# A hybrid attention block on one core: where the weights' sums, the tokens' sums and the rows of x are asked for

## The chip, the core and the metric

The kernel runs on one core of a Trainium2 chip. The core has a matrix engine (PE, with its weight loads as PEld), a vector engine (DVE), a scalar engine (ACT), GpSimd (POOL) and SyncE (SP), which here only issues transfers. The metric is the device time of one execution in microseconds (us); less is better.

## What is computed

One layer of a streaming encoder, 512 tokens, width 2048, eight stick-breaking heads and eight latent heads, all float32. Cut to what matters:

```
h = rms_norm(x, pre_norm_w)
sb_q, sb_k, sb_v, sb_gate, c_q, c_kv, k_rope, mla_gate = split(h @ w_in)
# stick-breaking heads (8 x 128), strictly causal
z = q @ k.T * scale
a[t,s] = sigmoid(z[t,s]) * prod_{s<j<t} (1 - sigmoid(z[t,j]))
o_a = a @ v
# latent heads (8): queries and keys by low-rank factors, rotary part, chunk-causal softmax
o_b = softmax(mask(q_mla @ k_mla.T * scale)) @ v_mla
mixed = concat([o_a * silu(sb_gate), o_b * silu(mla_gate)])     # 512 x 2048
y = mixed @ w_out                                               # 512 x 2048
out = x + rms_norm(y, post_norm_w)
```

## The kernel before, in words

**Products.** A float32 product is made of three products of parts: `split` (L94) makes a rounded part on ACT (L96, tiles ending in h or hi) and the remainder on DVE (L99, ending in l or lo), and `mm3` (L127) issues three matmuls (L122). `weights` (L104) brings a 128 x 1024 piece of a weight by a load on SP (L88, tile raw, four buffers) and splits it into whi and wlo (three buffers each).

**Order.** PE's matmuls and SP's loads are kept in the order of the code. On DVE, ACT and POOL a scheduler puts the instructions in an order by the place in the code and by when it takes their inputs to be ready, unless the code pins one with `keep_in_program_order`. Once built, each engine works through its list in order, so an instruction that waits holds all behind it.

**The run.** First the norm and the low-rank projections; then eight latent heads (to about 310 us), then eight stick-breaking heads (to about 700 us). A generator, `filler`, fills PE between the steps of the heads with the projections of the heads to come and, in the end, with the output product. In a stick-breaking head k is scaled (kr) and split (kh, kl); for each of four blocks b of 128 tokens there follow the scores z on PE, a mask on z (DVE, L885), two sigmoids (ACT, L887 the first), a scan (DVE, prod, L889), and a product (DVE, beta, L891). PE then transposes beta (tp) and multiplies it with v (av). The gated head, mix (L745), is put into DRAM by POOL (`put_aside`, L749) and comes back by `split_mixed` (POOL load L392, tile mx, then mxh and mxl).

**The output product.** The columns of w_out come in four groups of 512 for the tokens' four blocks. `out_group(0)` and `out_group(1)` (L433) take the first 1024 columns, eight weights i each with two mixed heads j; their four banks y are emptied by `out_piece`: a sum of squares on ACT (L407) and a product with the post weight on DVE (L416). The second group uses the same banks, so PE waits for L416 of the first. `last_columns` (L517) makes the other 1024 columns with seven products of half the size in place of eight, in the manner of Strassen: A11, S1, S2, S3, A22, A12 and, with weights kept from earlier, S4 (banks sx, sz, sy, sv, sx, sp). It needs sums on both sides:

- weights' sums: `weight_sums(j)` (L461), eight sets, each of four loads of 128 x 512 from w_out (POOL, L466, tile wsum, from a ring qrt of eight slots), four subtractions (DVE, L468) and four stores to DRAM (POOL, L469, tensors w_sums). They are called from the stick-breaking heads but depend on nothing there, and none is pinned;
- tokens' sums: `first_sums(j)` (L476), eight of them, called inside the output groups from the fifth weight of the first one on: two mixed heads again from DRAM (POOL, L473, ring mv of four slots), three sums (L481 to L483), splits (s12, hl4); and `last_sum` (L489), eight, in the second half of the second group.

S3 and A22 share the banks sv and are emptied by `sum_piece` (L419): L423 adds, L407 squares, L425 multiplies. Between A22 and A12, four pieces w22 are loaded and split into kept tiles (woh, wol, halves of 128 x 512) for S4; A12's own pieces are w21. `residual(b)` (L567) loads four pieces of x for a block (SP, tile xr), makes the factor r (L575, L576 on DVE, L578, L579 on POOL), computes x + r*y (L587) and stores it (L588, SP and ACT by turns).

Of the kernel before, what the change touches and what calls it, by code (L numbers as in the profile page):

```python
# [57 lines left out]
def block(ctx: ExitStack, tc: tile.TileContext, a: dict):  # L58
# [10 lines left out]
    def g(name, dt=F32, tag="g"):  # L69
        return gen.tile([P, S], dt, tag=tag, name=name, bufs=SLOTS[tag])  # L70
# [16 lines left out]
    def load(out, in_):  # L87
        tc.keep_in_program_order(nc.sync.dma_start(out=out, in_=in_))  # L88
# [15 lines left out]
    def weights(src, n):  # L104
        raw = ring.tile([P, 1024], F32, tag="raw", name="raw", bufs=N_RAW)
        load(out=raw[:, :n], in_=src)
        hi = ring.tile([P, 1024], F32R, tag="whi", name="whi", bufs=N_HI)
        lo = ring.tile([P, 1024], F32R, tag="wlo", name="wlo", bufs=N_HI)
        split(hi[:, :n], lo[:, :n], raw[:, :n])
        return hi, lo  # L110
# [322 lines left out]
    def out_group(gi):  # L433
        banks = [bank(f"y{b}") for b in range(NB)]
        for i in range(8):
            wh, wl = weights(a["w_o"][gi, i], 1024)
            if i == 0:
                for _ in range(4):
                    split_mixed()
            if 4 <= 8 * gi + i < 12:  # L440
                first_sums(8 * gi + i - 4)
            for j in range(2):
                s_ = slice(j * S, (j + 1) * S)
                split_mixed()
                for b in range(NB):
                    out_mm(banks[b], b, i * 2 + j, wh[:, s_], wl[:, s_])
                    yield
            if gi == 1 and i >= 4:
                last_sum(2 * i - 8)
                last_sum(2 * i - 7)  # L450
        pw = post_weight(gi)
        for b in range(NB):
            out_piece(b, gi * S, banks[b], pw)
# [4 lines left out]
    sums = {}  # L458
    w_sums = [dram.tile([4, P, 1024], F32, name=f"w_sums{n}") for n in range(4)]

    def weight_sums(j):  # L461

        i, c = j // 2, slice((j % 2) * S, (j % 2 + 1) * S)
        b11, b12, b22, b21 = (g("wsum", tag="qrt") for _ in range(4))
        for t, gi, k in ((b11, 2, 0), (b12, 3, 0), (b22, 3, 4), (b21, 2, 4)):
            pool.dma_start(out=t, in_=a["w_o"][gi, k + i][:, c])  # L466
        for n, (out, x, y) in enumerate(((b11, b12, b11), (b12, b22, b12), (b22, b22, b11), (b21, b21, b22))):
            dve.tensor_tensor(out=out, in0=x, in1=y, op=ALU.subtract)  # L468
            pool.dma_start(out=w_sums[n][i][:, c], in_=out)  # L469

    def mixed_again(n):
        t = g("mx", tag="mv")
        pool.dma_start(out=t, in_=mixed[order[n]])  # L473
        return t

    def first_sums(j):  # L476

        x, y = mixed_again(j), mixed_again(j + 8)
        t, s4 = g("st", tag="tr"), g("st4", tag="tr")[:, :HALF]
        s1, s2 = t[:, :HALF], t[:, HALF:]  # L480
        dve.tensor_tensor(out=s1, in0=x[:, HALF:], in1=y[:, HALF:], op=ALU.add)  # L481
        dve.tensor_tensor(out=s2, in0=s1, in1=x[:, :HALF], op=ALU.subtract)
        dve.tensor_tensor(out=s4, in0=y[:, :HALF], in1=s2, op=ALU.subtract)  # L483
        h12, l12, hl4 = g("s12h", F32R), g("s12l", F32R), g("s4", F32R)
        split(h12, l12, t)
        split(hl4[:, :HALF], hl4[:, HALF:], s4)
        sums[j] = h12, l12, hl4

    def last_sum(j):  # L489

        x = mixed_again(j)
        s3 = x[:, HALF:]
        dve.tensor_tensor(out=s3, in0=x[:, :HALF], in1=s3, op=ALU.subtract)
        split(msplit[j][0][:, HALF:], msplit[j][1][:, HALF:], s3)

    def factor(which, j, r):

# [6 lines left out]
        k, c = {"A11": (0, lo_), "S3": (0, hi_), "A12": (8, lo_), "A22": (8, hi_)}[which]  # L504
        return msplit[j + k][0][:, c], msplit[j + k][1][:, c]

    def product(banks, which, srcs, start, stop):
        for i in range(4):
            wh, wl = weights(srcs[i], 1024)
            for j in (2 * i, 2 * i + 1):  # L510
                s_ = slice((j % 2) * S, (j % 2 + 1) * S)
                for r in range(2):
                    mm3(banks[r], *factor(which, j, r), wh[:, s_], wl[:, s_], start and j == 0, stop and j == 7,
                        skip_group_check=True)
                    yield

    def last_columns():  # L517
        w11, w21, w22 = ([a["w_o"][gi, k + i] for i in range(4)] for gi, k in ((2, 0), (2, 4), (3, 4)))
        x = [bank("sx") for _ in range(2)]
        yield from product(x, "A11", w11, True, False)  # L520
        s1 = [g("s1", tag="t") for _ in range(2)]
        s15 = [g("s15", tag="t") for _ in range(2)]
        for r in range(2):
            act.copy(out=s1[r], in_=x[r])
        z = [zbank("sz") for _ in range(2)]
        yield from product(z, "S1", w_sums[0], True, True)
        for r in range(2):
            dve.tensor_tensor(out=s15[r], in0=z[r], in1=s1[r], op=ALU.add)
        y = [tbank("sy") for _ in range(2)]
        yield from product(y, "S2", w_sums[2], True, True)  # L530
        for r in range(2):
            dve.tensor_tensor(out=s1[r], in0=y[r], in1=s1[r], op=ALU.add)
            dve.tensor_tensor(out=s15[r], in0=y[r], in1=s15[r], op=ALU.add)
        pw2, pw3 = post_weight(2, "mv"), post_weight(3, "mv")
        junk = g("junk", tag="mv")
        v = [bank("sv") for _ in range(2)]
        yield from product(v, "S3", w_sums[1], True, False)
        for r in range(2):
            sum_piece(2 + r, 3 * S, v[r], s15[r], pw3, junk)
        yield from product(v, "A22", w_sums[3], False, True)  # L540
        for r in range(2):
            sum_piece(2 + r, 2 * S, v[r], s1[r], pw2, junk)

# [21 lines left out]
            residual(b, b == 1)  # L565

    def residual(b, tail=False):  # L567
        xs = []
        for i in range(4):
            xr = g("xr")  # L570
            load(out=xr, in_=a["x"][b * P:(b + 1) * P, i * S:(i + 1) * S])
            xs.append(xr)
        n = pieces[b]
        part = tn("part")
        dve.tensor_reduce(out=part, in_=ssy[b][:, :n - 1], axis=AX.X, op=ALU.add)  # L575
        dve.tensor_scalar(out=part, in0=part, scalar1=EPS, scalar2=None, op0=ALU.add)  # L576
        r2 = tn("r2")
        pool.tensor_tensor(out=r2, in0=ssy[b][:, n - 1:n], in1=part, op=ALU.add)  # L578
        pool.tensor_tensor(out=r2, in0=r2, in1=mhalf[:, :1], op=ALU.pow)  # L579
        for i, (at, y) in enumerate(sorted(ypw[b].items())):  # L580
            w = y.shape[1]
            o = xs[at // S][:, at % S:at % S + w]
            if tail and i == 2:
                act.activation(out=y, in_=y, func=AF.Copy, scale=r2)
                pool.tensor_tensor(out=o, in0=y, in1=o, op=ALU.add)
            else:
                dve.scalar_tensor_tensor(out=o, in0=y, scalar=r2, in1=o, op0=ALU.mult, op1=ALU.add)  # L587
            (nc.sync, nc.scalar)[i % 2].dma_start(out=a["out"][b * P:(b + 1) * P, at:at + w], in_=o)  # L588
# [283 lines left out]
        fill(max(0, 4 * NK + NK * (h + 2) - taken[0]))  # L872


    for h in range(H):
        kh, kl = need("k", h)
        qh, ql = need("q", h)
        fill(4)
        rows = row_tiles("beta")
        for b in range(NB):  # L880
            n = (b + 1) * P
            w = max(n, 256)
# [7 lines left out]
                                   initial=1.0, op0=ALU.mult, op1=ALU.add)  # L890
            dve.tensor_tensor(out=beta[:, :n - 1], in0=beta[:, :n - 1], in1=prod[:, 1:n], op=ALU.mult)  # L891
            fill((1, 3, 3, 7)[b])
        if h < H - 1:
            weight_sums(h)
        if h == H // 2:
            weight_sums(H - 1)
        cur = Weighted(rows, need("v", h // 4), (h % 4) * P)
        for j in range(NB):
            cur.turn(j)
# [64 lines left out]
```

## Time and profile before

| what | us |
| --- | --- |
| runs | 881.47, 881.5, 883.67; median 881.5 |
| profiled execution | 883.35 |
| span of the profiled execution | 881.3 |
| PE busy | 844.3 (96%) |
| PEld, DVE, ACT, POOL busy | 706.7, 485.3, 360.4, 91.2 |

A profile page gives the busy time of each engine, the span in slices, the transfers and the chain of work that ended last. Behind it the trace can be asked for stretches, waits and single instructions. In a row of the timeline the first number is the start, the second how long it took, then the engine, the line, the operation, the tile written and the tiles read; in brackets stands how long the engine was idle before and what it waited for. A line of waits names the engine with the waiting instruction, then what released it. A granted clock of 1.00 is PE's full speed, 2.4 GHz, and 0.50 is 1.2 GHz.

### The profile page before, as it was taken

How to read it: one execution, taken by the hardware profiler on the slowest of the kernel's cores; microseconds unless marked ns; L12 is line 12 of the kernel's file. 1: busy time of each engine (PE TensorE's matmuls, PEld its weight loads, DVE VectorE, ACT ScalarE, POOL GpSimd, SP SyncE). 2: the span in 40 equal slices, each digit the busy share in tenths (PEclk: the TensorE clock that was granted, in tenths of full speed). 3: DMA queues.
4: the chain of work that ended last, by engine and by line, in shares of the span. 5: the costliest groups of instructions: out<-in, count | busy, mean ns of one | idle time of the engine just before them, and what ended most of it. 6: DMA issues, size and time to landing. Idle time of an engine off the chain costs nothing.

```text
span 881.3 us, 11034 instructions
## 1 busy us (share of the span) xinstructions
PE 844.3 (96%) x4074; PEld 706.7 (80%) x4074; DVE 485.3 (55%) x869; ACT 360.4 (41%) x622; POOL 91.2 (10%) x189
## 2 busy tenths in 40 slices
PE   8999999988899999999999999999999996999993
PEld 6889988876688888888888888888888884888773
DVE  5676656657685543355363524546355666435675
ACT  7652655543444533333242324333244333334541
POOL 1000001134450020000000000000001021000011
PEclk9999999999899999999999999999999997999997
DMA  9822322356782152222323234222223275427677
GB/s 337 323 93 80 122 88 99 105 198 236 235 286 96 60 180 96 96 88 92 101 80 107 73 108 144 96 84 90 90 96 132 94 229 167 142 90 229 197 260 241
DMA packets 41477, 126.84 MB, mean 144 GB/s; under 512 B 5760, under 2 KB 6288, under 8 KB 41424
## 3 DMA queue, kind: packets, MB, share of 16 engines
q1 hardware_dynamic: 29520, 88.75, 30.0%
q0 software_dynamic: 10608, 35.42, 11.8%
q10 hardware_dynamic: 1296, 1.97, 0.6%
q8 instruction: 32, 0.52, 0.3%
q14 instruction: 21, 0.17, 0.1%
HBM read 109.34 MB, written 16.78 MB: 143 GB/s over the span
## 4 chain that ended last, share of the span: by engine, by line
PE 77%; DMA 10%; issue 5%; DVE 4%; ACT 2%; POOL 1%; SPq 1%; DVEq 0%; POOLq 0%; ACTq 0%
PE gps L122 16%; PE qp L122 10%; PE v L122 10%; PE kp L122 10%; PE y L122 6%; PE cq L122 4%; DMA wsum<-in_w_o 4%; PE av L122 3%; DMA xr<-in_x 2%; PE ckv L122 2%; PE sv L122 2%; DMA mx<-mixed 2%; PE mz L122 2%; PE z L122 2%; PE tp L125 2%
## 5 line engine op out<-in xcount | busy, mean ns | idle before, releaser
L99 DVE TENSOR_TENSOR wlo<-raw,whi 128x1024 fp32r<-128x1024 f32 (+2 forms) x137 | 163.3, 1192 | 144.1 <-ACT whi L96 141.3
L96 ACT CAST whi<-raw 128x1024 fp32r<-128x1024 f32 (+2 forms) x137 | 140.5, 1026 | 215.3 <-PE kp L122 42.6
L122 PE MATMUL gps<-hh,whi 128*128 128x512 f32 x256 | 102.9, 402 | 0.0
L122 PE MATMUL gps<-hl,whi 128*128 128x512 f32 x256 | 100.8, 394 | 0.0
L122 PE MATMUL gps<-hh,wlo 128*128 128x512 f32 x256 | 100.8, 394 | 0.0
L122 PE MATMUL y<-whi,mxh 128*128 128x512 f32 x128 | 51.3, 401 | 8.7 <-DVE y L416 8.7
L122 PEld LDWEIGHTS gps<-hh,wlo 128*128 128x128 f32 x256 | 48.5, 189 | 10.8
L122 PEld LDWEIGHTS gps<-hl,whi 128*128 128x128 f32 x256 | 48.8, 191 | 7.8
L122 PEld LDWEIGHTS gps<-hh,whi 128*128 128x128 f32 x256 | 48.6, 190 | 7.7
L96 ACT CAST th<-tp 128x512 fp32r<-128x512 f32 (+1 forms) x64 | 27.1, 423 | 66.0 <-PE tp L125 63.2
L99 DVE TENSOR_TENSOR tl<-tp,th 128x512 fp32r<-128x512 f32 (+1 forms) x64 | 31.2, 487 | 38.7 <-ACT th L96 38.2
L122 PE MATMUL qp<-hh,whi 128*128 128x512 f32 x128 | 52.0, 407 | 0.0
L122 PE MATMUL v<-whi,hh 128*128 128x512 f32 x128 | 50.9, 397 | 0.0
L122 PE MATMUL y<-wlo,mxh 128*128 128x512 f32 x128 | 50.8, 397 | 0.0
L122 PE MATMUL y<-whi,mxl 128*128 128x512 f32 x128 | 50.7, 396 | 0.0
L122 PE MATMUL qp<-hh,wlo 128*128 128x512 f32 x128 | 50.1, 391 | 0.0
L122 PE MATMUL qp<-hl,whi 128*128 128x512 f32 x128 | 50.0, 391 | 0.0
L122 PE MATMUL v<-whi,hl 128*128 128x512 f32 x128 | 49.9, 390 | 0.0
L122 PE MATMUL v<-wlo,hh 128*128 128x512 f32 x128 | 49.9, 390 | 0.0
L122 PE MATMUL kp<-hh,whi 128*128 128x512 f32 x128 | 49.8, 389 | 0.0
L122 PE MATMUL kp<-hl,whi 128*128 128x512 f32 x128 | 49.8, 389 | 0.0
L122 PE MATMUL kp<-hh,wlo 128*128 128x512 f32 x128 | 49.8, 389 | 0.0
(290 smaller groups left out, 1806.8 us busy)
## 6 DMA issues: line engine op xcount, KB each, us to landing
raw<-in_w_t SPq DMA_DIRECT2D x64, 512.0 KB, 3.2
raw<-in_w_o SPq DMA_DIRECT2D x28, 512.0 KB, 3.2
mx<-mixed POOLq DMA_DIRECT2D x39, 256.0 KB, 3.7
wsum<-in_w_o POOLq DMA_DIRECT2D x32, 256.0 KB, 3.7
w_sums<-wsum POOLq DMA_DIRECT2D x32, 256.0 KB, 2.9
raw<-in_w_v SPq DMA_DIRECT2D x16, 512.0 KB, 3.2
raw<-w_sums SPq DMA_DIRECT2D x16, 512.0 KB, 4.3
xs<-in_x SPq DMA_DIRECT2D x16, 256.0 KB, 6.4
```

Of the source, the lines that this page charges most:

```text
L96: i = act.copy(out=hi, in_=src)
L99: dve.tensor_tensor(out=lo, in0=src, in1=hi.bitcast(F32), op=ALU.subtract)
L122: tc.keep_in_program_order(pe.matmul(out=out, lhsT=lhsT, rhs=rhs, start=start, stop=stop, **kw))
L125: tc.keep_in_program_order(pe.transpose(out, in_, identity))
```

## The change

Three things, in one diff.

1. `weight_sums` is cut in two: `load_weight_parts` at the head of a stick-breaking head, the subtractions and stores behind its four blocks; all of it is pinned. Head h has set h, head 4 has set 7 as well. The four sums are stored in another order (the tensors 1 and 2 change places, and S2 and S3 read accordingly).
2. `first_sums` is called two weights earlier in the code, its loads one step ahead of it; the last sums become a generator, `late_sums`, that is stepped beside A11 and S1. Neither is pinned.
3. The rows of x are loaded by `load_x`, a generator stepped beside S3 (blocks 2 and 3) and A22 (blocks 0 and 1): two loads of 256 KB behind each piece of weights, on SP, pinned. `residual` finds them there.

```diff
-            if 4 <= 8 * gi + i < 12:
-                first_sums(8 * gi + i - 4)
+            at = 8 * gi + i - 6
+            if 0 <= at + 1 < H:
+                load_pair(at + 1)
+            if 0 <= at < H:
+                first_sums(at)
...
-            if gi == 1 and i >= 4:
-                last_sum(2 * i - 8)
-                last_sum(2 * i - 7)
...
+    def load_weight_parts(j):
+        i, c = j // 2, slice((j % 2) * S, (j % 2 + 1) * S)
+        w_parts[j] = []
+        for gi, k in ((2, 0), (3, 0), (3, 4), (2, 4)):
+            t = g("wsum", tag="qrt")
+            tc.keep_in_program_order(pool.dma_start(out=t, in_=a["w_o"][gi, k + i][:, c]))
+            w_parts[j].append(t)
+
     def weight_sums(j):
...
+        b11, b12, b22, b21 = w_parts.pop(j)
+        for n, (out, x, y) in ((0, (b11, b12, b11)), (2, (b12, b22, b12)), (1, (b22, b22, b11)), (3, (b21, b21, b22))):
+            tc.keep_in_program_order(dve.tensor_tensor(out=out, in0=x, in1=y, op=ALU.subtract))
+            tc.keep_in_program_order(pool.dma_start(out=w_sums[n][i][:, c], in_=out))
...
+    def load_pair(j):
+        pairs[j] = mixed_again(j), mixed_again(j + 8)
...
+    def late_sums():
+
+        xs = [mixed_again(j) for j in range(2)]
+        for j in range(H):
+            x = xs.pop(0)
+            s3 = x[:, HALF:]
+            dve.tensor_tensor(out=s3, in0=x[:, :HALF], in1=s3, op=ALU.subtract)
+            split(msplit[j][0][:, HALF:], msplit[j][1][:, HALF:], s3)
+            if j + 2 < H:
+                xs.append(mixed_again(j + 2))
+            yield
...
+    def load_x(b0):
+
+        for b in (b0, b0 + 1):
+            x_rows[b] = []
+            for i in range(4):
+                xr = g("xr")
+                load(out=xr, in_=a["x"][b * P:(b + 1) * P, i * S:(i + 1) * S])
+                x_rows[b].append(xr)
+                if i % 2:
+                    yield
...
-    def product(banks, which, srcs, start, stop):
+    def product(banks, which, srcs, start, stop, beside=iter(())):
         for i in range(4):
             wh, wl = weights(srcs[i], 1024)
+            next(beside, None)
...
-        yield from product(x, "A11", w11, True, False)
+        sums_of = late_sums()
+        yield from product(x, "A11", w11, True, False, sums_of)
...
-        yield from product(v, "S3", w_sums[1], True, False)
+        yield from product(v, "S3", w_sums[2], True, False, load_x(2))
...
-        yield from product(v, "A22", w_sums[3], False, True)
+        yield from product(v, "A22", w_sums[3], False, True, load_x(0))
...
-        xs = []
-        for i in range(4):
-            xr = g("xr")
-            load(out=xr, in_=a["x"][b * P:(b + 1) * P, i * S:(i + 1) * S])
-            xs.append(xr)
+        xs = x_rows[b]
...
+    w_todo = [[h] for h in range(H - 1)] + [[]]
+    w_todo[H // 2].append(H - 1)
     for h in range(H):
...
+        for j in w_todo[h]:
+            load_weight_parts(j)
...
-        if h < H - 1:
-            weight_sums(h)
-        if h == H // 2:
-            weight_sums(H - 1)
+        for j in w_todo[h]:
+            weight_sums(j)
```

On POOL the 32 loads and 32 stores of the weights' sums, and on DVE their subtractions, stood among the instructions of the latent heads, and nothing stands in their place there. Line numbers move by up to 31: the last sums are L508, the subtractions are L476 and the stores L477 in the changed kernel, the mask, the scan and the product L918, L922 and L924, the put L778, the residual step L616.

**DVE in stick-breaking head 4**, from the split of k on, before:

```order
L99 TENSOR_TENSOR kl<-kr,kh 128x512
L885 TENSOR_TENSOR z<-z,m_sb 128x128
L889 SCALAR_TENSOR_TENSOR prod<-keep,zero 128x128
L891 TENSOR_TENSOR beta<-beta,prod 128x127
L885 TENSOR_TENSOR z<-z,m_sb 128x128
L889 SCALAR_TENSOR_TENSOR prod<-keep,zero 128x256
L891 TENSOR_TENSOR beta<-beta,prod 128x255
L99 TENSOR_TENSOR wlo<-raw,whi 128x1024
L885 TENSOR_TENSOR z<-z,m_sb 128x128
```

And now, from the same instruction on:

```order
L99 TENSOR_TENSOR kl<-kr,kh 128x512
L476 TENSOR_TENSOR wsum<-wsum 128x512 x2
L918 TENSOR_TENSOR z<-z,m_sb 128x128
L476 TENSOR_TENSOR wsum<-wsum 128x512
L922 SCALAR_TENSOR_TENSOR prod<-keep,zero 128x128
L918 TENSOR_TENSOR z<-z,m_sb 128x128
L924 TENSOR_TENSOR beta<-beta,prod 128x127
L476 TENSOR_TENSOR wsum<-wsum 128x512
L922 SCALAR_TENSOR_TENSOR prod<-keep,zero 128x256
L476 TENSOR_TENSOR wsum<-wsum 128x512
L924 TENSOR_TENSOR beta<-beta,prod 128x255
L476 TENSOR_TENSOR wsum<-wsum 128x512
```

Eight subtractions stand among the masks, scans and products of this head; in the other heads that have one set the first four of them stand at the same places.

**DVE at the step from the first to the second group of the output product** (st, s12l and s are a pair's sums and splits, the last sums L493 in one kernel and L508 in the other, L416 empties the banks), before:

```order
L99 TENSOR_TENSOR wlo<-raw,whi 128x1024
L99 TENSOR_TENSOR s_6621<-st_6615,s_6621 128x256
L482 TENSOR_TENSOR st<-st,mx 128x256
L493 TENSOR_TENSOR mx<-mx 128x256
L483 TENSOR_TENSOR st_6661<-mx,st 128x256
L493 TENSOR_TENSOR mx<-mx 128x256
L99 TENSOR_TENSOR s12l<-st,s12h 128x512
L99 TENSOR_TENSOR s_6667<-st_6661,s_6667 128x256
L493 TENSOR_TENSOR mx<-mx 128x256
L99 TENSOR_TENSOR wlo<-raw,whi 128x1024
L493 TENSOR_TENSOR mx<-mx 128x256
L416 TENSOR_TENSOR y_6494<-y_6040,pw 128x512
```

And now:

```order
L494 TENSOR_TENSOR st<-mx 128x256
L508 TENSOR_TENSOR mx<-mx 128x256
L495 TENSOR_TENSOR st<-st,mx 128x256
L496 TENSOR_TENSOR st_6721<-mx,st 128x256
L508 TENSOR_TENSOR mx<-mx 128x256
L99 TENSOR_TENSOR s12l<-st,s12h 128x512
L99 TENSOR_TENSOR s_6727<-st_6721,s_6727 128x256
L99 TENSOR_TENSOR wlo<-raw,whi 128x1024
L508 TENSOR_TENSOR mx<-mx 128x256 x2
L99 TENSOR_TENSOR wlo<-raw,whi 128x1024
L416 TENSOR_TENSOR y_6466<-y_6040,pw 128x512
```

Four of the last sums stand ahead of the first L416 in both; what moved is that the two remainders (wlo) ahead of it now stand behind all of the last pair's sums.

**ACT at the end of A22 and the start of A12**, before (woh are casts of kept weights, whi here casts of A12's w21, L407 with ssy_590 and ssy_591 the epilogue of A22):

```order
L96 CAST woh<-raw 128x512 x6
L96 CAST whi<-raw 128x1024 x2
L407 ACTIVATE junk,ssy_590<-y_7267 128x512
L96 CAST whi<-raw 128x1024
L407 ACTIVATE junk,ssy_591<-y_7271 128x512
L96 CAST whi<-raw 128x1024
```

And now:

```order
L96 CAST woh<-raw 128x512 x7
L407 ACTIVATE junk,ssy_590<-y_7299 128x512
L96 CAST woh<-raw 128x512
L407 ACTIVATE junk,ssy_591<-y_7303 128x512
L96 CAST whi<-raw 128x1024 x4
```

The first casts for A12 stood ahead of the epilogue, and stand behind it now.

**DVE at the same place**, before:

```order
L99 TENSOR_TENSOR wol<-raw,woh 128x512 x2
L423 TENSOR_TENSOR y_7267<-sv,s_6948 128x512
L99 TENSOR_TENSOR wlo<-raw,whi 128x1024
L423 TENSOR_TENSOR y_7271<-sv,s_6949 128x512
L425 TENSOR_TENSOR y_7267<-y_7267,pw 128x512
L99 TENSOR_TENSOR wlo<-raw,whi 128x1024
```

And now:

```order
L99 TENSOR_TENSOR wol<-raw,woh 128x512 x5
L423 TENSOR_TENSOR y_7299<-sv,s_6932 128x512
L423 TENSOR_TENSOR y_7303<-sv,s_6933 128x512
L99 TENSOR_TENSOR wol<-raw,woh 128x512
L425 TENSOR_TENSOR y_7299<-y_7299,pw 128x512
L99 TENSOR_TENSOR wol<-raw,woh 128x512
L425 TENSOR_TENSOR y_7303<-y_7303,pw 128x512
L99 TENSOR_TENSOR wol<-raw,woh 128x512
L99 TENSOR_TENSOR wlo<-raw,whi 128x1024 x3
```

The remainder (wlo) for A12's first weights stood between the two additions L423, and stands behind all of the epilogue now.

## Rows read from the trace of the kernel before

**Rows 1.** Stretches: us, busy us (instructions) by engine, granted clock, DMA share, GB/s.
```profile
20.00:38.00 18.00, 18.00 (x81) 14.89 (x80) 9.72 (x12) 15.51 (x34) 0.00 (x0) 1.00 1.04 409
154.73:262.65 107.92, 98.70 (x481) 81.33 (x481) 71.34 (x152) 47.94 (x91) 39.58 (x78) 0.95 0.62 211
262.65:309.60 46.95, 46.95 (x249) 40.14 (x249) 27.37 (x63) 24.27 (x46) 3.57 (x9) 1.00 0.24 86
733.65:742.38 8.73, 0.00 (x2) 0.00 (x1) 6.56 (x14) 5.32 (x12) 1.10 (x2) 0.71 0.39 128
742.38:747.24 4.86, 4.86 (x12) 3.79 (x13) 2.87 (x4) 0.00 (x0) 0.00 (x0) 0.50 0.51 156
831.45:843.50 12.05, 11.67 (x52) 9.15 (x50) 10.68 (x18) 8.69 (x15) 0.00 (x0) 1.00 0.72 233
867.50:881.30 13.80, 0.00 (x0) 0.00 (x0) 6.70 (x13) 1.74 (x5) 2.04 (x3) 0.61 0.73 248
```

**Rows 2.** DVE's waits from 154 to 263 us; then the view of tile wsum.
```profile
DVE wsum L468 <- DMA wsum<-in_w_o: 21.4, 12, 3.6
...
L468 DVE TENSOR_TENSOR wsum<-wsum x32: 680/692/695, 153.5 to 262.7; 128x512 f32<-128x512 f32 x32
...
DMA to landing us min/median/max: 2.2/3.6/6.3
```

**Rows 3.** PE's waits over the whole span: total us, times, longest us.
```profile
PE y L122 <- DVE y L416: 8.7, 1, 8.7
```

**Rows 4.** Timeline of stick-breaking heads 6 and 7: DVE, PE, POOL, DVE (start, us).
```profile
640.12 0.30 DVE L885 TENSOR_TENSOR z<-z,m_sb 128x128 f32<-128x128 f32 x1 [1.07 <-PE z L122]
640.86 0.42 DVE L889 TENSOR_TENSOR_SCAN prod<-keep,zero 128x128 f32<-128x128 f32 x1 [0.44 <-ACT keep L887]
...
649.85 0.69 DVE L891 TENSOR_TENSOR beta<-beta,prod 128x511 f32<-128x511 f32 x1
...
651.07 0.60 PE L125 MATMUL tp<-ident,beta 128*128 128x128 f32 x4
...
663.55 0.54 POOL L749 DMA_DIRECT2D mixed<-mix  x1 [5.88 <-DVE mix L745]
...
676.15 0.69 DVE L99 TENSOR_TENSOR kl<-kr,kh 128x512 fp32r<-128x512 f32 x1
```

**Rows 5.** DVE's waits from 686 to 745 us; timeline of DVE, then SP's queue.
```profile
DVE st L481 <- DMA mx<-mixed: 9.2, 4, 4.4
...
707.32 0.43 DVE L481 TENSOR_TENSOR st<-mx 128x256 f32<-128x256 f32 x1 [1.76 <-DMA mx<-mixed]
...
725.50 0.43 DVE L481 TENSOR_TENSOR st<-mx 128x256 f32<-128x256 f32 x1 [4.44 <-DMA mx<-mixed]
...
741.64 1.28 DVE L416 TENSOR_TENSOR y<-y,pw 128x512 f32<-128x512 f32 x2
...
714.69 0.33 SPq L88 DMA_DIRECT2D pw<-in_post_w  x1
```

**Rows 6.** Timeline of the tail: DVE, then POOL.
```profile
869.65 0.75 DVE L423 TENSOR_TENSOR y<-sp,s 128x256 f32<-128x256 f32 x2
...
873.81 0.75 DVE L587 SCALAR_TENSOR_TENSOR xr<-y,r,xr 128x512 f32<-128x512 f32 x1 [2.04 <-DMA xr<-in_x]
...
876.08 1.40 DVE L587 SCALAR_TENSOR_TENSOR xr<-y,r,xr 128x256 f32<-128x256 f32 x2 [0.54 <-DMA xr<-in_x]
...
871.89 0.54 POOL L579 TENSOR_TENSOR r<-r,mhalf 128x1 f32<-128x1 f32 x1
```

**Rows 7.** Timeline at the start of A12: ACT, DVE, PE.
```profile
842.50 1.05 ACT L96 CAST whi<-raw 128x1024 fp32r<-128x1024 f32 x1 [1.11 <-DMA raw<-in_w_o]
...
845.44 0.63 ACT L407 ACTIVATE junk<-y 128x512 f32<-128x512 f32 x1
...
843.03 0.69 DVE L423 TENSOR_TENSOR y<-sv,s 128x512 f32<-128x512 f32 x1 [0.83 <-PE sv L122]
...
844.91 0.50 PE L122 MATMUL sx<-wlo,mxh 128*128 128x512 f32 x1 [0.81 <-DVE wlo L99]
```

More of the change, by code (lines that the diff above doesn't have):

```diff
@@ L459, in block @@
     w_sums = [dram.tile([4, P, 1024], F32, name=f"w_sums{n}") for n in range(4)]
+    w_parts = {}
+    def load_weight_parts(j):
[5 more added lines that the diff above has]
+            w_parts[j].append(t)
     def weight_sums(j):
         i, c = j // 2, slice((j % 2) * S, (j % 2 + 1) * S)
[L464 to L469, printed above, removed]
+        b11, b12, b22, b21 = w_parts.pop(j)
+        for n, (out, x, y) in ((0, (b11, b12, b11)), (2, (b12, b22, b12)), (1, (b22, b22, b11)), (3, (b21, b21, b22))):
+            tc.keep_in_program_order(dve.tensor_tensor(out=out, in0=x, in1=y, op=ALU.subtract))
+            tc.keep_in_program_order(pool.dma_start(out=w_sums[n][i][:, c], in_=out))
     def mixed_again(n):
@@ L474, in mixed_again @@
         return t
+    pairs = {}
+    def load_pair(j):
+        pairs[j] = mixed_again(j), mixed_again(j + 8)
     def first_sums(j):
-        x, y = mixed_again(j), mixed_again(j + 8)
+        x, y = pairs.pop(j)
         t, s4 = g("st", tag="tr"), g("st4", tag="tr")[:, :HALF]
@@ L487, in first_sums @@
         sums[j] = h12, l12, hl4
[L489 to L494, printed above, removed]
+    def late_sums():
[8 more added lines that the diff above has]
+            yield
+    x_rows = {}
+    def load_x(b0):
[7 more added lines that the diff above has]
+                    yield
     def factor(which, j, r):
@@ L525, in last_columns @@
         z = [zbank("sz") for _ in range(2)]
-        yield from product(z, "S1", w_sums[0], True, True)
+        yield from product(z, "S1", w_sums[0], True, True, sums_of)
         for r in range(2):
@@ L529, in last_columns @@
         y = [tbank("sy") for _ in range(2)]
-        yield from product(y, "S2", w_sums[2], True, True)
+        yield from product(y, "S2", w_sums[1], True, True)
         for r in range(2):
```

## Prediction

> **What bounds the kernel now.** The page comes first: its first line, in the table above, has PE busy for 96% of the span. So there is little to take from PE's work, and the change removes none of it: PE's instructions and their order stay as they are. What can be won is the time in which PE stands still or runs at half clock, and the tail behind its last matmul. The table of stretches says where these lie, and there the reader should compare PE's busy time with the length of each stretch [rows 1].
>
> First place: the four latent heads that carry the weights' sums take 107.92 us; two latent heads without them, in the stretch behind, take 46.95 us at full clock [rows 1]. Four at that pace take 93.90 us, so the stretch loses 14.02 us: 107.92 - 98.70 = 9.2 us in which PE is idle, and the rest of it in a mean clock of 0.95. What makes them idle is told by DVE's waits there: 21.4 us, in 12 waits, for the DMA that brings the parts of w_out to the subtractions (L468) [rows 2]. DVE works in order, so a mask, a cast's remainder or a softmax step behind such a subtraction is late by as much.
>
> Second place: PE's longest wait of all, 8.7 us for L416 [rows 3]. It is the step from the first to the second group of output columns, 733.65 to 742.38, and behind it 4.86 us run at clock 0.50 [rows 1]. At full clock the twelve matmuls of those 4.86 us would take half of them, so the half clock costs 2.4 us and the place 11.1 us.
>
> Third place: behind the last matmul (867.50) lie 13.80 us in which PE has nothing left [rows 1], and DVE's rows there show waits for rows of x [rows 6].
>
> **Baseline.** The profiled span is 881.3 us, and the profiled execution 883.35 us; the median of the runs is 881.5. The sum is a difference within the span, and I take it off the median.
>
> **Part 1, the weights' sums leave the latent heads.** The 32 loads, 32 subtractions and 32 stores are gone from there, and nothing takes their place on POOL or DVE. What then remains is the work of the heads on either side: -14.0 us (from -13 to -14.2, as the neighbours may wait a little themselves).
>
> In the stick-breaking heads PE never waits now, and the cover is DVE's gaps. DVE's chain of a head ends with the last beta (649.85 + 0.69 = 650.54), and PE takes that beta at 651.07, so 0.5 us are to spare [rows 4]. A set is four subtractions of 0.69 us (0.65 from one start to the next, an estimate) [rows 2], 2.8 us. Two stand ahead of the first mask, where DVE waits 1.07 us for PE; one stands ahead of the first scan, with a wait of 0.44 us for ACT; one ahead of the second [rows 4]. Each gap swallows most of what stands in it: 2 x 0.65 - 1.07 = 0.2, 0.65 - 0.44 = 0.2, and 0.1 behind it, 0.5 us late in all, just what is to spare. Six heads with one set: about 0.3 us together. In head 4 there are two sets; of the second, one fills the gap ahead of the fourth scan, and of the others about 1.2 us stay, for which there is no gap: +1.2. Head 6 also gets four splits of mixed heads that now stand among its own casts on ACT: I put +1.0, one split of 0.65 us and a wait, an estimate. Sum +2.5, from 0 (all in gaps) to +5 (a half-clock stretch of 2.4 us behind the stall in head 4).
>
> The loads' landing is no part of this: they stand on POOL right behind the previous head's put, 663.55 for the last head, and that head's kl comes at 676.15, 12 us later [rows 4]; the loads landed within 2.2 to 6.3 us [rows 2].
>
> **Part 2, the tokens' sums.** In the code they go two weights earlier, and the last ones behind the step. On DVE they hardly move: four of the last sums still stand ahead of L416, as they did. What changes is the data. Three splits of mixed heads are done in the last head, so slots are free and the first two pairs are there when the sums begin; and SP's load of the post weight now waits for the first pair's split, not the third's. In the trace of before it went out at 714.69 after a long wait, with the raw weights in a bunch behind it, and the pair beside them came at 725.50, after a wait of 4.44 us [rows 5]. DVE's waits for pairs are 9.2 us in all [rows 5]. Without the 4.44 us and the first (1.76 us) DVE reaches L416 at 741.64 - 6.20 = 735.44 [rows 5], 1.8 us behind PE's last matmul of the group (733.65); the 3.0 us of waits for pairs that are left shrink too, as the pairs start a round earlier. I take 0.6 us of stall, and no half clock: -10.5 us. Bounds: -11.1 (no stall), -6 (the 4.44 us stay, and the half clock with them in part).
>
> **Part 3, the rows of x.** 16 loads of 256 KB go from the tail to beside the products S3 and A22. The tail: DVE's L423 for the last rows starts at 869.65, 2.15 us behind the last matmul, because the residual steps ahead of it on DVE waited for x; and the last residual steps wait for x again, 2.04 us at 873.81 and 0.54 us at 876.08 [rows 6]. With x there: the second L423 starts about 867.6 instead of 870.0, the factor r is ready 2.4 us behind it as now (870.0 to 872.43) [rows 6], four residual steps take 0.75 + 0.75 + 1.40 = 2.9 us, and from the last one's end to the span's end it is 881.3 - 877.48 = 3.8 us as now. That is 876.7 on this trace's time: -4.6; I put -4.7, as part of r is made sooner, from -3.5 to -5.2.
>
> The price of it is at A12, the product behind A22, and it is not a transfer but an order. Now ACT casts A12's first weights at 842.50 as soon as they land, ahead of the epilogue of A22 (L423, L407), and DVE's remainder stands between its two L423: A12's second matmul starts at 844.91, with a wait of 0.81 us [rows 7]. In the changed order all of the epilogue, with two casts of the kept weights among it, stands ahead of that cast on ACT and ahead of the remainder on DVE. Worked from rows: L423 at 843.03 as now, ready 843.7; L407 0.63; a half cast 0.6 (an estimate, from 1.05 for a whole one); the second L407 0.63: 845.6. Then the cast 1.05: 846.65, and the remainder, behind L425 and another half remainder, at 846.9 to 848.1 [rows 7]. A12's second matmul starts 3.2 us later than it does now, and a wait over 3 us has so far brought half clock behind it where the one of 0.81 did not: at the group's step it cost 2.4 us [rows 1]. I count 2.0 for it: +5.2. Bounds: +2.5 (no half clock, half casts done earlier), +8 (the weights land late as well).
>
> **The transfers of x.** Beside S3 and A22, eight steps of 2.72 us, 512 KB of sums and 512 KB of x are wanted in each: 1.05 MB / 2.72 us = 386 GB/s. Early in the kernel the queues moved 409 GB/s over 18 us; beside A22, per full share of the engines, 233 / 0.72 = 324 [rows 1]. By the first the transfers keep up; by the second the 8.4 MB take 25.9 instead of 21.8 us. I take the first, since it is a stretch where they were full, and count nothing; the other is a rival below. The Trainium skill, page "DMA: Bandwidth & Descriptors", section "Specifications", gives about 358 GB/s as the limit of one core's share of HBM: by it the loads would take 8.4 MB / 358 GB/s = 23.4 us, 1.7 us more than there are, and the sum would be 861.7 us. The row with 409 GB/s speaks against that limit here.
>
> **Sum.** -14.0 + 2.5 - 10.5 - 4.7 + 5.2 = -21.5 us: 881.5 - 21.5 = 860.0 us.
>
> **The rivals.** (a) A12's weights are not late, because the cast gets its turn between the epilogue's waits: 860.0 - 5.2 = 854.8. Against it: ACT works in order, and the order is fixed. Chance 0.10. (b) The tokens' sums keep PE waiting at the group's step, since in DVE's order they still stand ahead of L416, so that part does not do what it says: 860.0 + 10.5 = 870.5 in full, 865 in half. For it: the place on DVE is the same, and the pairs still have only two rounds of slots. Chance 0.12. (c) The x rows crowd out the weights: 25.9 - 21.8 = 4.1 us late where nothing hides it, about 862 to 864, as the raw buffers hold some steps ahead. For it: 324 per full share beside A22. Chance 0.15. (d) Slower: the subtractions in the stick-breaking heads wait for their DMA as they did in the latent ones. Part 1 without its +2.5 and parts 2 and 3 give -24.0, so eight sets must cost over 3.0 us each. A stall of 1.2 us with 2.4 us of half clock behind it would: 8 x 3.6 = 28.8, 881.5 - 24.0 + 28.8 = 886.3 us. The point from which it decides is a landing later than the first mask needs, over 12 us behind the issue, twice the longest seen. Chance 0.02. (e) Stalls of this kind in two or three heads only, and nothing won at the tail: within 0.3% would need 19 us more than I count; 0.02.
>
> **How the numbers follow.** The forecast as worked out has 0.59, and 860.0 us. The range reaches from (a), less a little, to (b) in half: 853 to 867. Faster by over 0.3% (2.6 us, about what a measurement of this kernel can tell from no change) are the forecast, (a), (b) and (c): 0.96; within it (e), 0.02; slower (d), 0.02.
>
> **What would show it.** Right: in the profile of after the four latent heads take 94 us at clock 1.00 and DVE has no wait for the parts of w_out there; PE's wait for L416 is under 1.5 us; a new wait of PE of some 3 to 5 us for the cast or the remainder of A12's first weights, with clock 0.5 behind it; the end some 20.5 us behind A12's end, not 25.2. Wrong: waits of PE for beta in every stick-breaking head (d), a wait for L416 over 5 us (b), ACT waiting for the DMA of sums in S3 and A22 (c).

## The result, and the profile after

The changed kernel takes 860.8 us in the median of its runs, the kernel before 882.59 us beside them; the ratio is 0.9745, with a 95% interval from 0.9721 to 0.9768. The forecast was 860.0 us, with a range from 853 to 867. The first profiled execution of the changed kernel ran at a lower clock from end to end; the rows below are from a later execution of the same kernel, measured together with the first experiments (860.73 us against 881.33 us; 0.9775, from 0.9753 to 0.9797). Its span is 859.9 us, against 881.3 us before.

The page's first lines: span, then busy us, share and instructions of each engine.

```profile
span 859.9 us, 11020 instructions
...
PE 838.3 (97%) x4074; PEld 704.6 (82%) x4074; DVE 484.4 (56%) x869; ACT 362.4 (42%) x622; POOL 90.8 (11%) x189
```

The sum over the places where PE does the same work in both kernels, from the starts of the same instructions in the two traces:

| from, to | before, us | after, us | difference | forecast |
| --- | --- | --- | --- | --- |
| start to the first matmul of the latent heads (mqp) | 107.54 | 107.81 | +0.3 | 0 |
| to kr of stick-breaking head 0 (latent heads) | 258.63 | 242.00 | -16.6 | -14.0 |
| to the first matmul of the output product (stick-breaking heads) | 320.64 | 324.96 | +4.3 | +2.5 |
| to the first of A11 (both output groups) | 101.64 | 90.35 | -11.3 | -10.5 |
| to the first of A12 | 55.15 | 58.21 | +3.1 | +5.2, with the next |
| to the first of S4 (A12) | 12.54 | 15.44 | +2.9 | |
| to the end (S4 and the tail) | 25.16 | 21.13 | -4.0 | -4.7 |
| span | 881.3 | 859.9 | -21.4 | -21.5 |

So each part went the way that was forecast, and the sizes were off by up to 2.6 us, in both directions.

Stretches of the profile after, with the columns of [rows 1]: the four latent heads, the first output group, the step to the second group, S3, A12, S4, and what lies behind the last matmul.

```profile
154.99:246.46 91.47, 91.47 (x482) 78.28 (x481) 55.21 (x122) 47.93 (x91) 7.10 (x18) 1.00 0.23 81
674.77:720.00 45.23, 45.23 (x208) 37.41 (x207) 33.76 (x63) 19.07 (x32) 10.58 (x21) 1.00 0.61 201
720.00:730.00 10.00, 10.00 (x46) 8.27 (x45) 5.44 (x9) 5.47 (x13) 1.09 (x2) 1.00 0.45 139
797.76:809.18 11.42, 11.04 (x49) 8.85 (x48) 7.74 (x10) 4.55 (x5) 0.00 (x0) 1.00 1.03 396
823.33:838.77 15.44, 14.00 (x49) 11.07 (x49) 10.99 (x16) 3.48 (x4) 0.74 (x2) 0.78 0.54 191
838.77:850.13 11.36, 11.35 (x73) 10.21 (x71) 5.66 (x11) 1.62 (x6) 1.23 (x2) 1.00 0.11 40
850.13:859.90 9.77, 0.00 (x0) 0.00 (x0) 4.81 (x10) 1.74 (x5) 2.52 (x3) 0.75 0.52 171
```

The first line answers to 107.92 us in [rows 1]: no idle time, and clock 1.00. The second and third have PE busy from end to end: the first matmul of the second group starts at 721.60, and there is no stretch like 733.65 to 742.38. The fourth shows the rows of x beside the sums: the transfer engines full, 396 GB/s, and 0.38 us of idle time at its end, for L423, as before. The fifth is the price at A12: clock 0.78. The last answers to 13.80 us.

The waits of PE over the whole span (total, times, longest), with those of the start, the first projections and two that are the same before (0.7 us in a latent head, 0.4 us for L423) left out:

```profile
PE sx L122 <- ACT whi L96: 3.0, 1, 3.0
PE z L122 <- ACT kh L96: 1.9, 1, 1.9
PE sx L122 <- DVE wlo L99: 1.4, 1, 1.4
...
PE z L122 <- DVE kl L99: 0.3, 1, 0.3
```

The wait for L416 of [rows 3] isn't among them any more. New are 2.98 and 1.44 us at A12, in place of 0.81, and 1.87 us, with 0.34 us behind it, in a stick-breaking head.

**A12.** ACT, DVE and PE, the rows that answer to [rows 7]:

```profile
820.49 0.63 ACT L407 ACTIVATE junk<-y 128x512 f32<-128x512 f32 x1 [2.05 <-DVE y L423]
...
821.12 0.60 ACT L96 CAST woh<-raw 128x512 fp32r<-128x512 f32 x1
821.62 0.62 ACT L407 ACTIVATE junk<-y 128x512 f32<-128x512 f32 x1
...
822.25 1.98 ACT L96 CAST whi<-raw 128x1024 fp32r<-128x1024 f32 x2
...
823.40 0.68 DVE L99 TENSOR_TENSOR wol<-raw,woh 128x512 fp32r<-128x512 f32 x1
824.00 2.35 DVE L99 TENSOR_TENSOR wlo<-raw,whi 128x1024 fp32r<-128x1024 f32 x2
...
823.33 0.50 PE L122 MATMUL sx<-whi,mxh 128*128 128x512 f32 x1 [2.98 <-ACT whi L96]
825.27 0.80 PE L122 MATMUL sx<-wlo,mxh 128*128 128x512 f32 x1 [1.44 <-DVE wlo L99]
825.86 0.63 PE L122 MATMUL sx<-whi,mxl 128*128 128x512 f32 x1
826.29 0.63 PE L122 MATMUL sx<-whi,mxh 128*128 128x512 f32 x1
```

The cast for A12's first weights comes at 822.25, when ACT has done both squares and the half cast between them; A22 had ended at 823.33 - 2.98 = 820.35. The remainder starts at 824.00, behind a half remainder. The matmuls behind it start 0.43 us apart, at about half of the pace: at clock 1.00 such matmuls start 0.23 us apart.

**A stick-breaking head.** POOL, ACT and DVE in head 6, up to its first scores (kr at 621.37):

```profile
610.93 1.62 POOL L468 DMA_DIRECT2D wsum<-in_w_o  x3 [0.43 <-issue]
612.70 1.15 POOL L392 DMA_DIRECT2D mx<-mixed  x2
621.11 1.18 POOL L392 DMA_DIRECT2D mx<-mixed  x2 [7.27 <-DVE mxl L99]
...
619.47 1.25 ACT L96 CAST mxh<-mx 128x512 fp32r<-128x512 f32 x2 [4.03 <-DMA mx<-mixed]
...
624.05 0.62 ACT L96 CAST mxh<-mx 128x512 fp32r<-128x512 f32 x1 [2.37 <-DMA mx<-mixed]
624.57 0.61 ACT L96 CAST kh<-kr 128x512 fp32r<-128x512 f32 x1
...
620.12 1.33 DVE L99 TENSOR_TENSOR mxl<-mx,mxh 128x512 fp32r<-128x512 f32 x2 [3.43 <-ACT mxh L96]
621.37 0.68 DVE L371 TENSOR_TENSOR kr<-kp,rstd_bc 128x512 f32<-128x512 f32 x1
...
625.22 0.69 DVE L99 TENSOR_TENSOR kl<-kr,kh 128x512 fp32r<-128x512 f32 x1 [2.04 <-ACT kh L96]
```

The first two of the mixed heads' loads (L392) were issued right behind those of the set (L468 in this kernel) and were not there before 619.4, nearly 7 us later. The next two went out at 621.11, when the remainders of the first had freed their buffers. ACT's casts waited for them 4.03 and 2.37 us, DVE's remainders with them, kr started 1.36 us late (39.14 us behind the last head's in place of 37.78), and kh, behind the cast that waited 2.37 us, at 624.57.

**The tail.** DVE and POOL, the rows that answer to [rows 6]:

```profile
850.00 0.75 DVE L423 TENSOR_TENSOR y<-sp,s 128x256 f32<-128x256 f32 x2
...
852.82 3.21 DVE L616 SCALAR_TENSOR_TENSOR xr<-y,r,xr 128x512 f32<-128x512 f32 x4 [0.71 <-POOL r L608]
...
852.23 0.55 POOL L608 TENSOR_TENSOR r<-r,mhalf 128x1 f32<-128x1 f32 x1
```

No wait of DVE for x is left. The second L423 starts at about 850.35, 0.2 us behind the last matmul, and the last residual steps take 3.21 us.

### The profile page after: what moved, and what is told of

It reads as the page before. It is cut to its first block, busy times and chain, and to the rows that moved or that the text cites. A ratio compares the mean times of both kernels' runs of the same rounds, so it can differ in the third digit from the quotient of the medians.

```text
span 1046.4 us, 11020 instructions
## 1 busy us (share of the span) xinstructions
PE 1031.2 (99%) x4074; PEld 761.8 (73%) x4074; DVE 492.0 (47%) x869; ACT 363.9 (35%) x622; POOL 90.8 (9%) x189
## 4 chain that ended last, share of the span: by engine, by line
PE 98%; DVE 1%; issue 0%; ACT 0%; POOL 0%; DVEq 0%; POOLq 0%; ACTq 0%
PE gps L122 21%; PE v L122 10%; PE y L122 10%; PE qp L122 10%; PE kp L122 10%; PE cq L122 5%; PE av L122 4%; PE mz L122 3%; PE sx L122 3%; PE sv L122 3%; PE mqp L122 3%; PE ckv L122 2%; PE tp L125 2%; PE z L122 2%; PE mv L122 1%; PE mkp L122 1%
## 5 line engine op out<-in xcount | busy, mean ns | idle before, releaser
L122 PE MATMUL gps<-hh,whi 128*128 128x512 f32 x256 | 119.2, 466 | 0.0
L122 PE MATMUL gps<-hl,whi 128*128 128x512 f32 x256 | 116.6, 456 | 0.0
L122 PE MATMUL gps<-hh,wlo 128*128 128x512 f32 x256 | 116.5, 455 | 0.0
L122 PE MATMUL qp<-hh,whi 128*128 128x512 f32 x128 | 60.5, 473 | 0.0
L122 PE MATMUL v<-whi,hh 128*128 128x512 f32 x128 | 59.8, 467 | 0.0
L122 PE MATMUL kp<-hl,whi 128*128 128x512 f32 x128 | 58.7, 458 | 0.0
L122 PE MATMUL qp<-hh,wlo 128*128 128x512 f32 x128 | 58.6, 458 | 0.0
L122 PE MATMUL v<-whi,hl 128*128 128x512 f32 x128 | 58.6, 457 | 0.0
L122 PE MATMUL kp<-hh,wlo 128*128 128x512 f32 x128 | 58.4, 456 | 0.0
L122 PE MATMUL qp<-hl,whi 128*128 128x512 f32 x128 | 58.4, 456 | 0.0
```

The costliest lines, as they stand in the source:

```text
L122: tc.keep_in_program_order(pe.matmul(out=out, lhsT=lhsT, rhs=rhs, start=start, stop=stop, **kw))
```

## The experiments

All times are medians in us; runs of the kernel before lie between 880.98 and 881.35 in the median.

**1. The change as it is.** 

> The changed kernel once more, for a profile at full clock. Theory: 860 us; four latent heads in 94 us at clock 1.00; PE's wait for L416 under 1.5 us; a new wait of PE of 3 to 5 us at the start of A12 with clock 0.5 behind it; 20.5 us from A12's end to the span's end. Rivals: no wait at A12 (a); L416 still waits for over 5 us (b); ACT waits for the DMA of sums in S3 and A22 (c).

Measured: 860.73 us. The four latent heads ran at clock 1.00, in 91.47 us in place of 94; the wait for L416 was gone; A12 had its waits, 2.98 and 1.44 us, with half clock behind them; from A12's end it was 21.1 us in place of 20.5. There is nothing of rivals (a) and (b). The sign of (c) stands there once: ACT waits 1.78 us for the DMA of a sum in S3. But the cast behind it starts at 803.52, which is 0.12 us later than the pitch of these casts (2.72 us behind 800.68), and PE has no wait for it.

**2. Part 1 alone.** The diff is `load_weight_parts`, `weight_sums` and `w_todo` as in the change, and nothing else.

> Part 1 alone: the weights' sums pinned to the stick-breaking heads, the rest as before. Theory: -14.0 in the latent heads and +2.5 in the stick-breaking heads, 870.0 us. Rival: the subtractions cost the stick-breaking heads what they cost the latent ones, 881.5 us, with waits of PE in each of the seven heads that have a set. If the stick-breaking heads hide all: 867.5 us.

Measured: 868.65 us against 881.33, ratio 0.9861 (0.9832 to 0.9889): -12.7 us. Waits of PE from 300 to 760 us:

```profile
PE y L122 <- DVE y L416: 8.2, 1, 8.2
PE z L122 <- ACT kh L96: 0.9, 1, 0.9
PE z L122 <- DVE kl L99: 0.3, 1, 0.3
PE av L122 <- DVE tl L99: 0.3, 1, 0.3
```

The wait for L416 is there as before, and of the stick-breaking heads only head 6 has waits, the longest 0.9 us for kh. The rival's wait in every head isn't there. In the trace the latent heads take 16.6 us less, as in the whole change, and the stick-breaking heads 2.4 us more, all of it from the kr of head 5 to that of head 7. That is 14.2 us in the traces and 12.7 in the medians, since the traced execution of the kernel before is one of its longer ones (883.35 us).

**3. Part 2 alone.** `first_sums` and `late_sums` as in the change.

> Part 2 alone: the tokens' sums with their loads a step ahead, the rest as before. Theory: PE's wait for L416 falls from 8.7 us to under 1.5 us and its half clock goes, -10.5 us, 871.0 us. Rival (b): the four last sums ahead of L416 keep it late, 876 to 881.5 us.

Measured: 872.65 us, 0.9910 (0.9891 to 0.9929): -8.7 us. The wait for L416 is 0.73 us, and the two output groups take 91.37 us in place of 101.64, -10.3 in the trace.

**4. Part 3 alone.** `load_x` as in the change.

> Part 3 alone: the rows of x beside S3 and A22, the rest as before. Theory: -4.7 in the tail and +5.2 at the start of A12, 882.0 us, no difference that can be measured; the trace shows both. Rival (a): nothing lost at A12, 876.8 us. Rival (c): the weights land late, 884 to 886 us.

Measured: 881.73 us, 1.0010 (0.9996 to 1.0024): no difference. PE's waits from 780 us on:

```profile
PE sx L122 <- ACT whi L96: 3.0, 1, 3.0
PE sx L122 <- DVE wlo L99: 1.1, 1, 1.1
```

The same two waits as in the whole change stand at A12. In the trace the way from A11 to A12 is 3.1 us longer, A12 2.4 us, the rest 4.0 us shorter. The three parts together are -12.7 - 8.7 + 0.4 = -21.0 us; the whole change was -20.6.

**5. and 6. Which half of part 2.** One kernel has the first sums moved and the loads a step ahead, the last sums as before. (In the expectations, as in the account of the change, I call this two weights earlier. It is later: the first pair is summed with the seventh weight instead of the fifth, and loaded with the sixth.)

```diff
-            if 4 <= 8 * gi + i < 12:
-                first_sums(8 * gi + i - 4)
+            at = 8 * gi + i - 6
+            if 0 <= at + 1 < H:
+                load_pair(at + 1)
+            if 0 <= at < H:
+                first_sums(at)
```

> Half of part 2 alone: the first sums two weights earlier in the code with their loads a step ahead, the last sums as before. Theory: the earlier loads are what takes the wait for L416 away, 872 to 873 us as with all of part 2. Rival: it needs the last sums behind the step, 878 to 881 us.

The other has the last sums beside A11 and S1, and the first sums as before.

> The other half of part 2 alone: the last sums stepped beside A11 and S1, the first sums as before. Theory: nothing, since four of them still stand ahead of L416: 881 us, wait for L416 about 8 us. Rival: 872 us.

Measured: 870.81 us, 0.9886 (0.9864 to 0.9907), with a wait of 0.93 us, and 881.11 us, 1.0000 (0.9986 to 1.0014). The first half does all of it; moving the last sums in the code does nothing, as the scheduler puts four of them ahead of L416 again. PE's wait for L416 in the one kernel, then in the other:

```profile
PE y L122 <- DVE y L416: 0.9, 1, 0.9
```

```profile
PE y L122 <- DVE y L416: 7.7, 1, 7.7
```

**7. Of that half, the two weights alone.**

```diff
-            if 4 <= 8 * gi + i < 12:
-                first_sums(8 * gi + i - 4)
+            if 6 <= 8 * gi + i < 14:
+                first_sums(8 * gi + i - 6)
```

> Of the first half of part 2, only the two weights earlier in the code, without loads a step ahead. Theory: it is this that puts pair 1 and the splits of three mixed heads ahead of the last stick-breaking head's end, and the post weight's load behind the first pair: 871 to 872 us. Rival: the loads a step ahead are needed: 876 to 881 us.

Measured: 872.37 us, 0.9892 (0.9854 to 0.9931), and a wait of 1.18 us for L416. Two numbers in the code are worth what all of part 2 is. With the sums later in the code, the scheduler puts the loads of three mixed heads for their splits, and those of pairs 0 and 1, ahead of the last head's put on POOL (678.54 to 687.24, the put at 701.90); before, only pair 0 and two of the mixed heads stood there (677.98 and 679.13, the put at 701.33). The four slots of the ring are then used by splits that can run before the last head is done, and not by a pair that waits for its turn on DVE. That this is how it works is read from the order; no run separates the slots from the rest of it.

**8. The order at A12.** The changed kernel, with two of A12's weights split ahead of A22's epilogue:

```diff
+        first = [weights(w21[i], 1024) for i in range(2)]
         for r in range(2):
             sum_piece(2 + r, 2 * S, v[r], s1[r], pw2, junk)
...
-        yield from product(x, "A12", w21, False, True)
+        yield from product(x, "A12", w21, False, True, first=first)
```

> The changed kernel, with A12's first two weights asked for and split ahead of A22's epilogue. Theory: the late start of A12 is an order on ACT and DVE alone; both its waits (2.98 and 1.44 us) go and the half clock behind them, 860.7 - 5.5 = 855 us, and A12 takes 12.6 us or less instead of 15.4. Rival: the weights land late beside the rows of x, and a wait of the same length comes back with a DMA as its releaser, 860 us.

Measured: 857.0 us, 0.9726 (0.9709 to 0.9743): -3.8 us of the 5.5. The trace of the kernel that has experiment 9's edit as well shows what is left: A12 starts without a wait, and its third weight makes PE wait.

```profile
PE sx L122 <- ACT whi L96: 1.5, 1, 1.5
PE sx L122 <- DVE wlo L99: 1.3, 1, 1.3
```

The load of that weight stands on SP behind those of the four kept weights. It went out at 820.81, when a kept weight's remainder on DVE had freed a buffer; ACT had done the kept weights' casts by 822.89 and waited 1.06 us more for it to land. So a DMA as the releaser, the sign of the rival, is there in small; what held it up in the trace is the order of the loads.

**9. No set in heads 5 and 6.** The changed kernel with

```diff
-    w_todo = [[h] for h in range(H - 1)] + [[]]
-    w_todo[H // 2].append(H - 1)
+    w_todo = [[0], [1, 5], [2], [3, 6], [4, 7], [], [], []]
```

> The changed kernel, with the sets of heads 5 and 6 moved to heads 1 and 3 (two sets each there, none in heads 5 and 6). Theory: a set costs a head nothing, two sets neither, and what costs 4.3 us is head 6, where mixed heads are loaded behind the set's loads and kr and kh wait for their splits: 860.7 - 4.3 = 856.4 us. Rival: two sets in one head cost 1.2 us and a half clock each, as I worked out for head 4: 860 us or more.

Measured: 858.54 us, 0.9739 (0.9720 to 0.9759): -2.2 us of the 4.3, and the interval still touches that of the changed kernel. PE's waits from 300 to 840 us:

```profile
PE y L122 <- DVE y L416: 0.8, 1, 0.8
PE av L122 <- DVE tl L99: 0.6, 1, 0.6
```

Heads 1 and 3 lost nothing with two sets each (37.80 and 81.32 us from one kr to the next, 37.78 and 81.30 before), and heads 5 and 6 are clean. But the scheduler now puts all eight early splits of mixed heads into head 4, which takes 1.3 us more, with the wait of 0.6 us; and the wait for L416 is back with 0.8 us. The first four splits take their buffers from the ring of the sets (tag qrt in `split_mixed`), and in both kernels the early splits stand with the last set, at 610 to 633 us (head 6) in the changed kernel and 553 to 570 us (head 4) here. That the ring ties them together is read from the code and the order; no run changes the ring.

**10. Both edits.** 

> Both of the two edits before. Theory: they lie apart, 860.7 - 5.5 - 4.3 = 851 us. Rival: one of them is undone by a new wait, 855 to 860 us.

Measured: 856.57 us, 0.9721 (0.9704 to 0.9738), which can't be told from experiment 8. The rival: the third weight's waits (above) take the place of those removed, and A12 takes 15.81 us in this trace, in place of 15.44. And of the 4.3 us at head 6, head 4 takes 1.4 and the wait for L416 0.8, nearly as in experiment 9.

**11. and 12. The third weight too.** The kept weights are asked for and split beside A12, a quarter with each of its weights (the loop over w22 becomes a generator `keep`):

```diff
-        yield from product(x, "A12", w21, False, True, first=first)
+        yield from product(x, "A12", w21, False, True, keep(), first)
```

> The changed kernel with the sets of heads 5 and 6 moved to heads 1 and 3, A12's first two weights split ahead of A22's epilogue, and the kept weights for S4 asked for and split beside A12, a quarter with each of its weights. Theory: with the third weight's cast no longer behind eight casts of kept weights, A12 has no wait over 0.8 us, and the time is that of both edits less 3 us, 853.5 us. Rival: S4 then waits for the last kept weights, 856 us or more.

> As the one before, with the sets two by two in heads 0 to 3, so that the splits of mixed heads come in two groups of four. Theory: the 1.3 us that head 4 loses with all eight splits in it go, 852.5 us. Rival: heads 0 to 3 lose as much, 854 us.

Measured: 852.41 us, 0.9678 (0.9663 to 0.9693), and 852.58 us, 0.9686 (0.9667 to 0.9704). Both beat the changed kernel by 8 us, and there is nothing between them: in the second 0.9 us are lost in head 0, with its two sets, and another 0.9 between the kr of heads 3 and 4, where all the early splits stand, in place of 1.2 in head 4. S3, then A12, in the trace of the first:

```profile
794.58:805.50 10.92, 10.92 (x49) 8.82 (x47) 7.24 (x9) 4.22 (x4) 0.00 (x0) 1.00 1.04 403
817.00:828.43 11.43, 11.43 (x50) 8.85 (x48) 10.56 (x16) 6.56 (x12) 1.25 (x2) 1.00 0.45 161
```

A12 takes 11.43 us at full clock. What is left of the waits of PE behind the first projections are 0.7, 0.7 and 0.4 us. The edit moves both the loads and the casts of the kept weights; which of the two the third weight needed isn't separated.

## Why the prediction was right, and where its sizes were off

**The latent heads** (-14.0, measured -16.6). The cause was right: in the stretch that answers to 107.92 us PE has no idle time and full clock. The step that was mis-sized is the pace. I took the two heads behind the stretch, 46.95 us, as the pace of the four. But the row of those two has 249 matmuls, and that of the four 481, 240.5 for two [rows 1]: by the count the four take 46.95 x 481 / 249 = 90.7 us, and they took 91.47. The number that sets the pace stood in the row that I read. The gain also differs from trace to trace: the way to kr of head 0 takes 242.0 to 242.1 us behind mqp in the six kernels without the sums in these heads, and in those with them 257.6 to 259.1, but 255.0 in experiment 5.

**The stick-breaking heads** (+2.5, measured +4.3). For six heads with one set I put 0.3 us, and for head 4 with its two 1.2: five of the seven pitches from one kr to the next are as before, 37.78 us (81.3 where values are projected), head 4's among them. DVE and PE in head 4 of the changed kernel, kr, the first subtractions, the last beta and its transpose:

```profile
544.45 0.69 DVE L371 TENSOR_TENSOR kr<-kp,rstd_bc 128x512 f32<-128x512 f32 x1 [3.35 <-PE kp L122]
...
547.05 1.41 DVE L476 TENSOR_TENSOR wsum<-wsum 128x512 f32<-128x512 f32 x2
...
558.03 0.69 DVE L924 TENSOR_TENSOR beta<-beta,prod 128x511 f32<-128x511 f32 x1
...
559.15 0.60 PE L125 MATMUL tp<-ident,beta 128*128 128x128 f32 x4
```

The last beta ends 14.27 us behind kr, in place of 650.54 - 636.37 = 14.17 in head 6 before: the eight subtractions fit into the gaps. The two other pitches, and the whole loss, belong to head 6, for which I had put 1.0 as an estimate: PE waits 1.87 + 0.34 us, and 2.1 us are lost at half clock. What waits there is neither a subtraction nor its transfer: it is ACT's casts of mixed heads, for loads queued behind the set's, in the middle of the kr and kh of that head. I had said that the loads' landing was no part of this; for the set's own loads that holds, as DVE has no wait for them, for the loads queued behind them it doesn't. Experiment 9 takes the set away from there, and head 6's wait is gone. It takes the splits away with it, so that the queue behind the set makes the loads late is read from the rows (6.8 us to landing, 3.4 in the median) and not shown by a run.

**The group's step** (-10.5, measured -11.3). The wait for L416 is gone altogether: DVE gets to it while the group's last matmuls still run (674.77 + 46.84 = 721.61), and waits for ACT.

```profile
720.48 2.79 DVE L416 TENSOR_TENSOR y<-y,pw 128x512 f32<-128x512 f32 x4 [0.75 <-ACT junk L407]
```

I had left 0.6 us of stall. The data came as I had it: the post weight's load went out 18.4 us behind the group's first matmul (693.12), in place of 27.9 (714.69), and DVE's waits for the pairs fell from 9.2 us to 2.5.

```profile
DVE st L494 <- DMA mx<-mixed: 2.5, 3, 1.5
```

That moving the last sums in the code does nothing, and the place of the first sums does all, is shown by experiments 5 to 7: in experiment 6 the post weight's load stays at 27.4 us and the waits at 7.8, in experiment 7 they are 18.2 and 5.8, with four of the last sums ahead of L416 in both. That it works by what stands earlier on POOL is read from the order. One thing about it I had read wrongly in the diff: the first sums are called two weights later in the code, not earlier. The working went by the order on the engines, which shows the loads and splits ahead of them, so the term wasn't touched.

**A12** (+5.2, measured +6.0). The order on ACT and DVE does it, shown by experiments 4, 8 and 11. My working had the cast done 3.15 us behind A22's end, and 2.98 us was the wait. It had the second matmul 3.2 us later than before; it came 3.6 later (825.27 - 820.35 = 4.92 us behind A22's end, in place of 1.31). The rest, 2.3 us net, is the half clock, for which I had 2.0.

**The tail** (-4.7, measured -4.0). The last residual steps take 3.21 us in place of the 2.9 that I had, and the second L423 comes 0.1 us later than I had it.

**The rivals.** (c), the rows of x crowding out the weights, isn't there: beside S3 the engines moved 396 GB/s at a share of 1.03, PE waits for no DMA in the products before A12 (ACT once does, which makes its cast 0.12 us late), and A12's first wait is for ACT, which was busy with the epilogue. The figure per full share from beside A22 (324) was the wrong one of the two rows: beside S3 it is 396 / 1.03 = 384, against 386 that were wanted, so there was little to spare. By the same row the limit of about 358 GB/s, which I cited from the Trainium skill, page "DMA: Bandwidth & Descriptors", section "Specifications", doesn't bind here: 396 GB/s went through with no wait of PE for a transfer. (d), waits for the set's loads in every head, isn't there either.

That the forecast hit the total by 0.8 us is in part luck: 2.6 us too little gain in the latent heads stand against 1.8 us too little loss in head 6, and 0.8 us too little gain at the group's step against 0.8 us too little loss at A12 and 0.7 us too much gain in the tail. The single terms are good to 1 to 3 us.

## What to carry to other kernels

When a stretch with a stall is compared with a clean one beside it, divide by the matmuls that each of them holds. When work is moved into a phase that hides it, look at what is queued behind its transfers as well as at the work itself, and at what a scheduler then puts into the same phase. And a pin for one thing moves others: here rows of x that were asked for earlier cost 6 us by the order in which two in-order engines came to the next weights; asking for these weights first, and for the kept ones later, gave it back.

## What the runs showed of the hardware

A wait of PE can cost more than its length. Behind waits of 0.73, 0.93 and 1.18 us at the group's step (experiments 3, 5 and 7), and behind 0.93 us in head 6 (experiment 2), the granted clock stayed at 1.00, which is 2.4 GHz. Behind 8.23 us (experiment 2) it was 0.57 over the next 5 us, and behind 1.87 and 0.34 us in head 6, as behind 2.98 and 1.44 us at A12, the next matmuls start 0.43 us apart, at 1.2 GHz. Behind 1.50 and 1.25 us at A12's third weight (experiment 10) it fell to 0.50, too. The stretch in head 6, with the columns of [rows 1]:

```profile
626.20:629.60 3.40, 3.40 (x12) 2.82 (x12) 3.40 (x9) 1.15 (x4) 2.17 (x4) 0.51 0.43 136
```

And the one behind the longest of the short waits:

```profile
735.40:741.00 5.60, 5.60 (x25) 4.62 (x26) 3.29 (x5) 0.99 (x3) 0.55 (x1) 1.00 0.58 190
```

So a wait over 3 us, by which I had decided at A12, is too high a mark: in the trace of before waits of 2.05, 2.90 and 2.75 us in the latent heads were followed by 0.50 as well. Nor does the length of the last wait decide it alone. The first of these three, at about 183 us, comes back in the kernels that leave the weights' sums in the latent heads: it was 2.05 us before, 2.01 in experiment 3 and 2.04 in experiment 7, with a mean clock of 0.62, 0.62 and 0.58 over the next 4 us, and 2.03 us in experiment 5 and 2.14 in experiment 4, with 1.00. No run here shows what decides between them.
